# Norm factors behind W_down and on the attention scores, query chunks first in W_in, input chunks straight into yT

## The chip, the cores and the metric

The kernel runs on one core of one Trainium2 chip. The time is the device time of one execution in microseconds; the kernel before has a median of 2802.93 us over three runs (2802.38 to 2804.43).

The engines are called by short names. PE is the matrix engine (PEld is its weight load, which overlaps with the matmuls), DVE the vector engine, ACT the scalar (activation) engine, POOL the GpSimd engine, and SP the engine whose queue issues most DMA transfers. PSUM is where matmuls write, SBUF is the working memory.

## The reference

The computation is a decoder of two layers over 1024 tokens of width 1024, all in f32. In one layer:

```
a  = rmsnorm(h, norm_mix_pre)                  # y * g * rsqrt(mean(y*y) + 1e-6), per token
u  = a @ w_in                                  # 1024 -> 2640 columns, split among the heads
q, k, v, qi, ki, wi, u_conv, u_pool = split(u) # qi: 16 index heads of 64, ki: one, wi: 16 weights
idx = sum_h relu(qi_h . ki) * wi_h             # per query and key; causal; times a constant
sel = top_k(idx, 256)                          # 256 keys per query
y_attn = softmax(q . k[sel] / 8) @ v[sel]      # 8 query heads, 2 key heads
mix = concat(y_attn, conv(u_conv), pool(u_pool)) @ w_out
h += rmsnorm(mix, norm_mix_post)
m  = square(relu(rmsnorm(h, norm_mlp_pre) @ w_up)) @ w_down      # 1024 -> 4096 -> 1024
h += rmsnorm(m, norm_mlp_post)
h += sigmoid(h @ ple_gate) * (p @ ple_proj)
```

Two identities matter here. The factor r = rsqrt(mean(h*h) + eps) of a token multiplies its whole row, so it can be taken through a linear map: (r x) W = r (x W). It is positive, so relu(r x)^2 = r^2 relu(x)^2. A choice of the largest index scores of a query is not altered by a positive factor on that query's row.

## The kernel before, in words

**Layout.** Activations lie with channels in the 128 partitions and tokens along the row, 512 tokens (a "half", `hf`) at a time. Every dense product is made of three passes of 128x512 matmuls, since both operands are split into a high and a low part: `whi`/`wlo` of the weights, and the two parts of a `slot` of the activations. One "unit" is one 128-column chunk of a weight matrix against 8 slots: 24 matmuls into one of three PSUM tiles `pd` (lines 252, 257, 258). Five more PSUM tiles, `bank`, belong to attention, convolution and pooling.

**Weights.** A chunk arrives from memory as `wraw` (SP queue, 512 KB), ACT makes `whi` (L213) and POOL makes `wlo` (L214) from it.

**Phases.** The list `PHASES` runs win(0,0), win(0,1), m(0,0), win(1,0), m(0,1), win(1,1), m(1,0), m(1,1), where the pair is (layer, half). A win phase is 21 units of W_in, named in `win_order`: M0, M1, MK (mixed heads of q, k and the index weights, the rotated part), I0 to I7 (index queries; I0 and I1 carry the rotated channels), V, Q0 to Q2 (queries), A/G (convolution) and P (pooling). An m phase is W_out, a norm, W_up and W_down in four groups of 8 units each, a norm, and the embedding gate.

**Factors in a win phase.** `rms_sb` sums squares by one-column matmuls (L307), computes the factor (DVE L318, POOL power L320), spreads it over the partitions by four transposes (L312) into a `pd` tile, and ACT copies it to `rb` in SBUF (L327). Each unit's result is then multiplied by `rb`: `scaled` (L355, on DVE), the rotation tables on POOL (L344). In the first half of the first layer `rb` is needed by the very first unit's evacuation, A0 at L397.

**Factors in W_up.** After the norm that follows W_out, the squares of the new h are summed at once, four W_up units run ahead with a plain Relu on ACT, then `rms_sb` makes `rb`, the four early tiles are multiplied by it (DVE L984), and every later unit is evacuated by one DVE instruction that takes the maximum with zero and multiplies by `rb` (L990), followed by a square on ACT (L991) and a split into high and low parts.

**Temporaries.** `dtmp` is a ring of 128x512 tiles that nearly every evacuation, table, square and input chunk draws from. An input chunk of x lands in a `dtmp`, is split (L274/L275), squared (L290) and given back. `yT` holds eight 128x512 chunks in f32 and is free during the win phases of the first layer.

**Order.** Attention and convolution are generators that are advanced between units: after each unit its cost times the phase's entry in `RATES` is spent on them. Attention of a half is put on that list after unit I7; an index step loads four heads of queries at a time (L617, on POOL's queue, from the memory tensor `qiS` that the I units wrote on SP's queue at L364), multiplies them with the keys (L610) and adds relu times weight into `idx` (ACT L651, DVE L655). At the start of an m phase whatever attention of that half is left runs alone. A scheduler then puts the instructions of each engine into one fixed order by its own estimate of when they can start; each engine runs its list strictly in order, and so does each DMA queue at issue.

Of the kernel before, what the change touches and what calls it, by code (L numbers as in the profile page):

```python
# [18 lines left out]
P = 128  # L19
# [15 lines left out]
RATES = (1.205, 1.114, 0.558, 0.766, 0.751, 0.567, 0.731, 0.946)  # L35
# [14 lines left out]
def win_order(l, hf):  # L50

    return WIN_CONV + WIN_ATT if CONV_FIRST[l][hf] else WIN_ORDER
# [34 lines left out]
def tile_trunk(ctx: ExitStack, tc: tile.TileContext, xT, pT, pos, vecs, invf, cinv,  # L87
# [10 lines left out]
    class Ring:  # L98
# [8 lines left out]
        def put(self, *tiles):  # L107
            self.free.extend(tiles)
# [63 lines left out]
    wiT = const.tile([P, DEPTH, 8, 16], F32, name="wiT")  # L172
    rbs = Ring("rb", 1, [P, HALF])
# [104 lines left out]
    class Sq:  # L278
# [20 lines left out]
        def rms(self, ps, other=None):  # L299
            rms(ps, self.acc, D, 1e-6, other)  # L300
            dtmp.put(*self.acc)

    def token_sums(ps, srcs):

        for j in range(4):
            for i, src in enumerate(srcs):
                te.matmul(ps[:, j:j + 1], src[:, j * P:(j + 1) * P], ones, start=i == 0, stop=i == len(srcs) - 1)  # L307
# [6 lines left out]
    def rms(ps, srcs, n, eps, other=None):  # L314

        token_sums(other or ps, srcs)
        v = tiny("rv")
        ve.tensor_scalar(v, (other or ps)[:, :4], 1.0 / n, eps, op0=OP.mult, op1=OP.add)  # L318
        r = tiny("rr")
        gp.tensor_tensor(r, v, mhalf, op=OP.pow)  # L320
        spread(ps, r)

    def rms_sb(sq):
        ps = pd.get()
        sq.rms(ps)
        rb = rbs.get()
        sc.activation(rb, ps, AF.Copy)  # L327
        pd.put(ps)
        return rb
# [4 lines left out]
    def win_phase(l, hf, xs, sq):  # L334
        t0 = hf * HALF
        ts = slice(t0, t0 + HALF)
        rb = rms_sb(sq)

        def table(t):
            out = []  # L340
            for i in range(2):
                x = dtmp.get()
                sy.dma_start(x, tabS[2 * t + i][:, ts])
                gp.tensor_tensor(x, x, rb, op=OP.mult)  # L344
# [39 lines left out]
        for name in win_order(l, hf):  # L384
# [29 lines left out]
            elif name in ("M0", "I0"):  # L414
                held = rope_first(ps, tab, P if name == "I0" else 88)
                if name == "M0":
# [5 lines left out]
                    sc.activation(wiT[:, l, 4 * hf:4 * hf + 4], pw[:, :64].rearrange("p (j h) -> p j h", j=4), AF.Copy)  # L422
# [173 lines left out]
    def attention(l, hf):  # L596
# [43 lines left out]
        def index():  # L640

            load_k(2, 0, Ws[-1])
            for j, b in enumerate(sel):
                W = Ws[j]
                for h in range(16):
                    if h % 4 == 0:
                        q = load_q(qiS, b, h, 16)
# [120 lines left out]
        def softmax(q, b, heads, k0, ring, out):  # L768
            W = (b + 1) * P
            bias = idx[sel.index(b)] if b in sel else cbias[:, 2 * P - W:]  # L770
            for g in heads:
                t = ring.get()
                mx, nm, rs, ri = tiny("mx", 2), tiny("nm", 1), tiny("rs", 1), tiny("ri", 1)
                for n0, n1, ps in scores(q[:, g], W, k0):
# [3 lines left out]
                    banks.put(ps)  # L778
                if W > 512:
                    ve.tensor_scalar(nm, mx[:, 0:1], mx[:, 1:2], -0.125, op0=OP.max, op1=OP.mult)  # L780
                else:
                    ve.tensor_scalar(nm, mx[:, 0:1], -0.125, None, op0=OP.mult)
                s = t[:, :W]
                sc.activation(s, s, AF.Exp, scale=0.125, bias=nm, accum_out=rs)  # L784
# [80 lines left out]
    def post_norm(sq, g, ts, hsrc, gnext, fill):  # L865
# [6 lines left out]
        sq.rms(ps, sums)  # L872
# [22 lines left out]
        if gnext is not None:  # L895
            for k in reversed(range(NK)):
                nxt.add(yT[:, k])
# [36 lines left out]
    def m_phase(l, hf):  # L934
# [32 lines left out]
        rb = None  # L967
        sqy = Sq()
        for gr in range(4):
            ms = []  # L970
            for u in range(8):
                if rb is None:

                    early = []
                    for k in range(4):
                        ps, t = unit(xs, k < 2), dtmp.get()
                        sc.activation(t, ps, AF.Relu)
                        pd.put(ps)
                        early.append(t)
                    rb = rms_sb(sq)  # L980
                m = slots.get()
                if early:
                    t = early.pop(0)
                    ve.tensor_tensor(t, t, rb, op=OP.mult)  # L984
                    sc.activation(t, t, AF.Square)
                    split(m[:, 0], m[:, 1], t)
                    dtmp.put(t)
                else:
                    ps = unit(xs)
# [183 lines left out]
```

## Time and profile before

| what | value |
|---|---|
| median of three runs | 2802.93 us |
| the profiled execution, device time | 2803.82 us |
| its span (first to last instruction) | 2802.1 us |
| PE busy | 2701.1 us, 96% |
| DVE, ACT, POOL busy | 1698.4, 1599.7, 1372.7 us |
| granted PE clock over the span | 0.986 |
| bytes moved | 380.63 MB, 136 GB/s on average |

Start and end of the phases in the profiled execution: the first index score matmul of win(0,0) starts at 152.28 us, the first W_out unit that needs attention of (0,0) at 378.93 us, the last norm at about 2739 us.

A line of a waits view reads "engine tile line <- the engine, tile and line that ended the wait: us in total, times, longest". A line of a windows view reads "from:to length, PE busy (number of matmuls), then PEld, DVE, ACT and POOL in the same way, granted PE clock, share of the DMA engines, GB/s". A line of a groups view reads "line, engine, operation, out<-in, shapes, count | busy us, mean ns | idle before it, and what ended that".

### The profile page before, as it was taken

Reading aid. Unit: us, or ns where it says so; the run is one execution under the profiler, and the core shown is the slowest. Engines: PE = TensorE matmul, PEld = TensorE weight load, DVE = VectorE, ACT = ScalarE, POOL = GpSimd, SP = SyncE. Lnnn points to the kernel's source line nnn. Section 1 sums busy time; section 2 is a strip of 40 time slices with the busy share of each in tenths; the row PEclk is TensorE's granted clock in tenths of the full one; section 3 lists DMA queues with packets and bytes.
Section 4 is the critical chain, followed back from the end, with each engine's and each line's share of the span. In section 5 each row is a group of like instructions: output and inputs, shape, how many; then the busy total and the mean of one; then the engine's idle time right before and its main releaser. Section 6 shows DMA issues by size and latency. Waiting matters only on the chain.

```text
span 2802.1 us, 37352 instructions
## 1 busy us (share of the span) xinstructions
PE 2701.1 (96%) x12512; PEld 2224.5 (79%) x12512; DVE 1698.4 (61%) x3399; ACT 1599.7 (57%) x3008; POOL 1372.7 (49%) x1085
## 2 busy tenths in 40 slices
PE   8889989999999999999999989999999999999998
PEld 6678877887888787788888778788878887788886
DVE  7869668678657868784422595676785561411123
ACT  5357668776766544685633434677757664533343
POOL 4655425444334674544344764444443346544446
PEclk9999999999999999999999999999999999999999
DMA  5677555432343566543333656533222354422223
GB/s 177 203 184 226 147 140 150 109 98 84 94 109 108 185 204 192 177 128 117 90 101 103 213 156 212 155 105 110 93 85 84 105 176 150 144 98 98 98 94 132
DMA packets 193425, 380.63 MB, mean 136 GB/s; under 512 B 17232, under 2 KB 76752, under 8 KB 193232
## 3 DMA queue, kind: packets, MB, share of 16 engines
q1 hardware_dynamic: 150992, 357.26, 39.8%
q0 software_dynamic: 42240, 20.98, 4.4%
q8 instruction: 99, 1.62, 0.2%
q14 instruction: 94, 0.77, 0.1%
HBM read 305.81 MB, written 72.35 MB: 135 GB/s over the span
## 4 chain that ended last, share of the span: by engine, by line
PE 78%; DVE 10%; DMA 5%; issue 2%; ACT 2%; POOL 1%; SPq 0%; POOLq 0%; ACTq 0%; DVEq 0%
PE pd L252 22%; PE pd L257 22%; PE pd L258 22%; PE bank L610 6%; PE bank L798 2%; DVE bank L549 2%; PE bank L807 1%; PE bank L806 1%; DMA wraw<-win 1%; DVE row L761 1%; DVE dtmp L884 1%; PE pd L255 1%; PE pd L307 1%; POOL wlo L214 1%; DVE dtmp L270 1%
## 5 line engine op out<-in xcount | busy, mean ns | idle before, releaser
L214 POOL TENSOR_TENSOR wlo<-wraw,whi 128x512 fp32r<-128x512 f32 x824 | 1097.4, 1336 | 1215.7 <-ACT whi L213 1147.0
L252 PE MATMUL pd<-slot,whi 128*128 128x512 f32 x3296 | 1305.6, 397 | 44.5 <-ACT whi L213 8.9
L258 PE MATMUL pd<-slot,wlo 128*128 128x512 f32 x3168 | 1245.4, 394 | 5.4 <-POOL wlo L214 5.1
L257 PE MATMUL pd<-slot,whi 128*128 128x512 f32 x3168 | 1245.8, 393 | 0.0
L213 ACT ACTIVATE whi<-wraw 128x512 fp32r<-128x512 f32 x824 | 512.8, 627 | 722.3 <-PE pd L257 520.2
L252 PEld LDWEIGHTS pd<-slot,whi 128*128 128x128 f32 x3296 | 625.1, 190 | 181.6 <-ACT whi L213 10.8
L258 PEld LDWEIGHTS pd<-slot,wlo 128*128 128x128 f32 x3168 | 600.1, 189 | 132.6 <-POOL wlo L214 9.2
L257 PEld LDWEIGHTS pd<-slot,whi 128*128 128x128 f32 x3168 | 600.6, 190 | 121.0 <-DVE slot L275 1.2
L610 PE MATMUL bank<-kd,qst 128*128 128x512 f32 (+3 forms) x1024 | 263.4, 361 | 15.6 <-DMA qst<-qiS 6.3
L655 DVE SCALAR_TENSOR_TENSOR idx<-bank,wiT,idx 128x512 f32<-128x512 f32 (+3 forms) x300 | 190.0, 652 | 89.1 <-ACT bank L651 80.8
L610 PEld LDWEIGHTS bank<-kd,qst 128*128 128x128 f32 x1024 | 181.2, 193 | 50.5 <-DMA qst<-qiS 7.2
L651 ACT ACTIVATE bank<-bank 128x512 f32<-128x512 f32 (+2 forms) x320 | 154.6, 506 | 71.5 <-PE bank L610 69.5
L1004 DVE TENSOR_TENSOR yT<-yT,pd 128x512 f32<-128x512 f32 x96 | 65.5, 684 | 203.7 <-PE pd L258 203.1
L990 DVE SCALAR_TENSOR_TENSOR pd<-pd,rb 128x512 f32<-128x512 f32 x112 | 78.0, 696 | 166.9 <-PE pd L258 166.6
L678 DVE TENSOR_SCALAR_CACHE_REDUCE row<-row,cc 128x640 f32<-128x640 uint16 (+1 forms) x124 | 133.5, 1078 | 63.4 <-ACT row L692 56.6
L549 DVE SCALAR_TENSOR_TENSOR bank<-win,vec,bank 128x512 f32<-128x512 f32 x232 | 165.5, 746 | 7.7 <-ACT bank L547 6.0
L776 DVE CUSTOM_DVE_ANT_0 row<-bank,idx 128x512 f32<-128x512 f32 (+3 forms) x160 | 91.7, 592 | 71.4 <-PE bank L610 50.4
L692 ACT ACTIVATE row<-row,cc 128x768 f32<-128x768 uint16 (+1 forms) x124 | 121.4, 982 | 22.9 <-DVE cc L698 20.5
L270 DVE TENSOR_TENSOR cmat<-bank,cmat 128x512 fp32r<-128x512 f32 (+1 forms) x160 | 98.3, 631 | 34.5 <-ACT cmat L269 30.9
L270 DVE TENSOR_TENSOR slot<-pd,slot 128x512 fp32r<-128x512 f32 x112 | 76.8, 687 | 52.8 <-ACT slot L269 52.5
L784 ACT ACTIVATE row<-row,nmc 128x384 f32<-128x384 f32 (+5 forms) x96 | 84.1, 877 | 36.0 <-DVE nmc L780 26.7
L269 ACT ACTIVATE cmat<-bank 128x512 fp32r<-128x512 f32 (+1 forms) x160 | 83.7, 546 | 26.4 <-PE bank L798 23.1
(216 smaller groups left out, 2724.1 us busy)
## 6 DMA issues: line engine op xcount, KB each, us to landing
wraw<-wup SPq DMA_DIRECT2D x128, 512.0 KB
wraw<-wdown SPq DMA_DIRECT2D x128, 512.0 KB
wraw<-win SPq DMA_DIRECT2D x84, 512.0 KB
qiS<-dtmp SPq DMA_DIRECT2D x64, 256.0 KB
slot<-mixS SPq DMA_DIRECT2D x32, 512.0 KB
wraw<-wgate SPq DMA_DIRECT2D x32, 512.0 KB
qst<-qiS POOLq DMA_DIRECT2D x48, 256.0 KB, 3.9
hS<-yT SPq DMA_DIRECT2D x48, 256.0 KB
```

The source lines that it names most:

```text
L213: sc.activation(hi, r, AF.Copy)
L214: gp.tensor_tensor(lo, r, hi.bitcast(F32), op=OP.subtract)
L252: te.matmul(ps, wh, xh, start=i == 0, stop=False)
L257: te.matmul(ps, wh, xl, start=False, stop=False)
L258: te.matmul(ps, wl, xh, start=False, stop=i == n - 1)
L270: ve.tensor_tensor(lo, src, hi.bitcast(F32), op=OP.subtract)
L549: ve.scalar_tensor_tensor(acc[:, c] if k == TAPS - 1 else pa, src, w, pa, op0=OP.mult, op1=OP.add)
L610: te.matmul(ps[:, :n1 - n0], q, kd[:, k, k0 + n0:k0 + n1], start=k == 0, stop=k == 1)
L651: sc.activation(r, r, AF.Relu)
L655: ve.scalar_tensor_tensor(at, r, w, at, op0=OP.mult, op1=OP.add)
L678: ve.tensor_scalar(flags[:, :Ws[j]], of[j], t, None, op0=op, op1=OP.add, accum_out=dst[:, j:j + 1])
L692: sc.activation(flags[:, :Ws[j]], of[j], AF.Sign, scale=-1.0, bias=c[:, j:j + 1], accum_out=cnt[:, j:j + 1])
```

## The change

1. **Win phases.** The factor of a token is kept as a column (`rq`, tokens in partitions). Query units Q0 to Q2 and I2 to I7 are written out without it (`scaled` gone from them). The rotated tables are multiplied only in rows 64 to 88 of the M tables, which are keys, and not at all for I0/I1. The index weights `wiT` get the factor when they are transposed: four small DVE instructions instead of one on ACT. The attention scores get it as the scale of the exponential and in the row maximum, from `rq`. The index score uses unscaled index queries: a positive factor per query does not alter a choice.
2. **Order of W_in.** Units I2 and I3 (and I4 in the first phase) come first, the others in the order they had.
3. **W_up and W_down.** No `rb`: a W_up unit is evacuated by a maximum with zero alone. The squares of h are added up during the first group of W_up units, and factor powers r^2 and r^4 are computed as columns (`reciprocal`); the norm behind W_down takes them in: variance times r^4, and the final factor times r^2. The early Relu units and their four transposes are gone.
4. **Input.** The chunks of x land in `yT` instead of in `dtmp`, all eight transfers of a half ahead of the splits.
5. **Token sums.** The two accumulated tiles are summed into columns of their own and added on DVE, instead of accumulating in PSUM.
6. **Index steps.** The first query load is issued before the first index step, and two empty steps are put ahead of it. Four entries of `RATES` differ.

```diff
-RATES = (1.205, 1.114, 0.558, 0.766, 0.751, 0.567, 0.731, 0.946)
+RATES = (1.205, 1.078, 0.558, 0.775, 0.751, 0.661, 0.731, 0.94)
...
-    return WIN_CONV + WIN_ATT if CONV_FIRST[l][hf] else WIN_ORDER
+    first = ['I2', 'I3', 'I4'] if l == hf == 0 else ['I2', 'I3']
+    order = WIN_CONV + WIN_ATT if CONV_FIRST[l][hf] else WIN_ORDER
+    return first + [n for n in order if n not in first]
...
+        def reciprocal(self, ps):
+            v, r2, r4 = tiny("rv"), tiny("r2", bufs=2), tiny("r4", bufs=2)
+            variance(ps, self.acc, D, 1e-6, v)
+            dtmp.put(*self.acc)
+            ve.reciprocal(r2, v)
+            ve.scalar_tensor_tensor(r4, r2, 1.0 / D, r2, op0=OP.mult, op1=OP.mult)
+            return r2, r4
...
+    def rms(ps, srcs, n, eps, other=None, factor=None, keep=None):
         v = tiny("rv")
-        ve.tensor_scalar(v, (other or ps)[:, :4], 1.0 / n, eps, op0=OP.mult, op1=OP.add)
-        r = tiny("rr")
+        if factor is None:
+            variance(other or ps, srcs, n, eps, v)
+        else:
+            sums = other or ps
+            token_sums(sums, srcs)
+            ve.tensor_tensor(v, sums[:, :4], factor[1], op=OP.mult)
+            w = tiny("rw")
+            ve.tensor_tensor(w, sums[:, 4:8], factor[1], op=OP.mult)
+            ve.scalar_tensor_tensor(v, w, eps, v, op0=OP.add, op1=OP.add)
+        r = tiny("rr") if keep is None else keep
         gp.tensor_tensor(r, v, mhalf, op=OP.pow)
+        if factor is not None:
+            ve.tensor_tensor(r, r, factor[0], op=OP.mult)
         spread(ps, r)
...
-                gp.tensor_tensor(x, x, rb, op=OP.mult)
+                if t == 1:
+                    gp.tensor_tensor(x[64:88], x[64:88], rb[64:88], op=OP.mult)
...
-                    sc.activation(wiT[:, l, 4 * hf:4 * hf + 4], pw[:, :64].rearrange("p (j h) -> p j h", j=4), AF.Copy)
+                    for j in range(4):
+                        ve.tensor_scalar(wiT[:, l, 4 * hf + j], pw[:, j * 16:(j + 1) * 16], rq[:, l, hf, 0, j:j + 1], None,
+                                         op0=OP.mult)
...
-                put(scaled(ps), [(0, P, qiS, P * int(name[1]))])
+                put(ps, [(0, P, qiS, P * int(name[1]))])
...
-                put(scaled(ps), [(0, P, qS, P + P * int(name[1]))])
+                put(ps, [(0, P, qS, P + P * int(name[1]))])
...
+            first = load_q(qiS, sel[0], 0, 16)
+            for _ in range(2):
+                yield None
...
-                sc.activation(s, s, AF.Exp, scale=0.125, bias=nm, accum_out=rs)
+                sc.activation(s, s, AF.Exp, scale=r, bias=nm, accum_out=rs)
...
-                    ve.scalar_tensor_tensor(ps, ps, 0.0, rb, op0=OP.max, op1=OP.mult)
-                    sc.activation(ps, ps, AF.Square)
-                    split(m[:, 0], m[:, 1], ps)
-                    pd.put(ps)
+                ve.tensor_scalar(ps, ps, 0.0, None, op0=OP.max)
+                sc.activation(ps, ps, AF.Square)
+                split(m[:, 0], m[:, 1], ps)
+                if gr == 0:
+                    sq.add(yT[:, NK - 1 - u], ps)
+                pd.put(ps)
...
-            h = dtmp.get()
+            h = yT[:, k]
             sy.dma_start(h, xT[k * P:(k + 1) * P, ts])
-            if k == 0 and hf == 0:
+            if k == 1 and hf == 0:
                 ready.append(prepare(coming.pop(0)))
+        for k in range(NK):
+            h = yT[:, k]
             x = slots.get()
             xs.append(x)
             split_g(x[:, 0], x[:, 1], h, vec[:, 0, V_MIX_PRE + k:V_MIX_PRE + k + 1])
             sq.add(h)
-            dtmp.put(h)
```

The change also moves instructions. On PE, at the first unit's evacuation, the order before is the following. Lines 252, 257 and 258 are dense matmuls, 307 the sums of squares, 312 the spread of the factor; `pd_138` and `pd_139` are units A0 and G0.

```order
L307 MATMUL pd_137<-ones,dtmp_108 128x1
L257 MATMUL pd_138<-slot_82,whi_94 128x512
L258 MATMUL pd_138<-slot_82,wlo_98 128x512
L257 MATMUL pd_139<-slot_82,whi_96 128x512
L258 MATMUL pd_139<-slot_82,wlo_100 128x512
L312 MATMUL pd_137<-ident,rrd_227 128x128 x4
L252 MATMUL pd_137<-slot_75,whi_93 128x512
L257 MATMUL pd_137<-slot_75,whi_93 128x512
```

In the changed kernel (lines 255, 260, 261 are the dense matmuls, 319 the sums, 324 the spread; `pd_138` and `pd_139` are now I2 and I3) the place of the spread is this, and the sums stand behind 22 dense matmuls instead of 44:

```order
L261 MATMUL pd_139<-slot_81,wlo_100 128x512
L255 MATMUL pd_139<-slot_82,whi_96 128x512
L260 MATMUL pd_139<-slot_82,whi_96 128x512
L261 MATMUL pd_139<-slot_82,wlo_100 128x512
L324 MATMUL pd_137<-ident,rq 128x128 x4
L255 MATMUL pd_138<-slot_75,whi_95 128x512
L260 MATMUL pd_138<-slot_75,whi_95 128x512
```

Four matmuls stood between the last sum and the spread before; now there are 26, and the tile behind the spread is I2's old one, which is free without a factor.

On SP, at the start of the program, the order before is this (`wraw` is a weight chunk, `xT` an input chunk of 256 KB):

```order
L1053 DMA dtmp_102<-xT 128x512
L208 DMA wraw_91<-win 128x1024
L1053 DMA dtmp_104<-xT 128x512
L1053 DMA dtmp_106<-xT 128x512
L1053 DMA dtmp_108<-xT 128x512
L1053 DMA dtmp_101<-xT 128x512
L208 DMA wraw_92<-win 128x1024
L1105 DMA fr<-invf 128x2
L476 DMA row_121<-wcp 128x256
L208 DMA wraw_91<-win 128x1024
```

and after the change this:

```order
L1078 DMA yT<-xT 128x512 x2
L211 DMA wraw_91<-win 128x1024
L1078 DMA yT<-xT 128x512 x6
L211 DMA wraw_92<-win 128x1024
L1131 DMA fr<-invf 128x2
L511 DMA row_121<-wcp 128x256
L1078 DMA yT<-xT 128x512 x3
L211 DMA wraw_91<-win 128x1024
L1078 DMA yT<-xT 128x512 x4
```

One more chunk of x stands ahead of the first weights and eight instead of five ahead of the second; the second half's chunks, which stood among the queries' writes, now stand around the third weights, and their splits moved into the first 40 rows of ACT and DVE.

Later on SP, where the queries of the first phase are written out, the order before mixes the second half's input chunks with the writes to `qiS`:

```order
L364 DMA qiS<-dtmp_107 128x512
L364 DMA qiS<-dtmp_101 128x512
L1053 DMA dtmp_101<-xT 128x512
L364 DMA qiS<-dtmp_104 128x512
L208 DMA wraw_92<-win 128x1024
L1053 DMA dtmp_107<-xT 128x512
L364 DMA qiS<-dtmp_105 128x512
L1053 DMA dtmp_104<-xT 128x512
L1053 DMA dtmp_105<-xT 128x512
L208 DMA wraw_91<-win 128x1024
L364 DMA qiS<-dtmp_109 128x512
L364 DMA qiS<-dtmp_108 128x512
```

and now there is nothing between them but weights, with the writes of V and Q0 behind them:

```order
L397 DMA qiS<-dtmp_103 128x512
L397 DMA qiS<-dtmp_106 128x512
L211 DMA wraw_91<-win 128x1024
L397 DMA qiS<-dtmp_108 128x512
L211 DMA wraw_92<-win 128x1024
L397 DMA qS<-dtmp_101 128x512
L397 DMA qS<-dtmp_105 128x512
L492 DMA vS<-dtmp_102 128x512
```

Each input chunk stood in a queue that runs in order and had to wait for a `dtmp` to come free; now none stands there. On PE, 24 dense matmuls (unit V) lie between I7 and the first index score before, and 48 (V and Q0) after.

More of the change, by code (lines that the diff above doesn't have):

```diff
@@ L297, in add, with rms @@
             self.n += 1
-        def rms(self, ps, other=None):
-            rms(ps, self.acc, D, 1e-6, other)
+        def rms(self, ps, other=None, factor=None, keep=None):
+            rms(ps, self.acc, D, 1e-6, other, factor, keep)
             dtmp.put(*self.acc)
+        def reciprocal(self, ps):
[5 more added lines that the diff above has]
+            return r2, r4
     def token_sums(ps, srcs):
-        for j in range(4):
-            for i, src in enumerate(srcs):
-                te.matmul(ps[:, j:j + 1], src[:, j * P:(j + 1) * P], ones, start=i == 0, stop=i == len(srcs) - 1)
+        for i, src in enumerate(srcs):
+            for j in range(4):
+                te.matmul(ps[:, 4 * i + j:4 * i + j + 1], src[:, j * P:(j + 1) * P], ones, start=True, stop=True)
     def spread(ps, t4):
@@ L646, in index @@
                     if h % 4 == 0:
-                        q = load_q(qiS, b, h, 16)
+                        q = first if j == h == 0 else load_q(qiS, b, h, 16)
                     w = wiT[:, l, b, h:h + 1]
@@ L862, in attention, with post_norm @@
             yield from attend(blocks, (0, 0), rows)
-    def post_norm(sq, g, ts, hsrc, gnext, fill):
+    def post_norm(sq, g, ts, hsrc, gnext, fill, factor=None):
         side[0] = "norm"
@@ L871, in post_norm @@
         ps = pd.get()
-        sq.rms(ps, sums)
+        sq.rms(ps, sums, factor)
         pd.put(sums)
@@ L971, in m_phase @@
             for u in range(8):
[L972 to L977, printed above, removed]
-                        pd.put(ps)
-                        early.append(t)
-                    rb = rms_sb(sq)
-                m = slots.get()
[L982 to L989, printed above, removed]
-                    ve.scalar_tensor_tensor(ps, ps, 0.0, rb, op0=OP.max, op1=OP.mult)
-                    sc.activation(ps, ps, AF.Square)
-                    split(m[:, 0], m[:, 1], ps)
-                    pd.put(ps)
+                m = slots.get()
+                ps = unit(xs, gr == 0 and u < 2)
+                ve.tensor_scalar(ps, ps, 0.0, None, op0=OP.max)
[4 more added lines that the diff above has]
+                pd.put(ps)
                 ms.append(m)
                 yield 5.2
+            if gr == 0:
+                ps = pd.get()
+                apart2 = sq.reciprocal(ps)
+                pd.put(ps)
             if gr == 3:
                 slots.put(*xs)
-                rbs.put(rb)
             for o in range(NK):
```

28 lines of the change are left out of this document (16 added, 12 removed).

## The prediction

> **What bounds the kernel now.** I read the page first, then the granted clock and matmul counts of stretches, then PE's waits stretch by stretch.
>
> ```profile
> PE 2701.1 (96%) x12512; PEld 2224.5 (79%) x12512; DVE 1698.4 (61%) x3399; ACT 1599.7 (57%) x3008; POOL 1372.7 (49%) x1085
> PE 78%; DVE 10%; DMA 5%; issue 2%; ACT 2%; POOL 1%; SPq 0%; POOLq 0%; ACTq 0%; DVEq 0%
> 2500.00:2550.00 50.00, 50.00 (x222) 41.42 (x221) 9.69 (x14) 16.72 (x28) 23.89 (x19) 1.00 0.28 95
> 0.00:36.08 36.08, 23.81 (x81) 17.12 (x82) 26.28 (x48) 21.10 (x35) 14.68 (x16) 0.86 0.55 182
> 36.08:104.00 67.92, 60.20 (x248) 47.53 (x247) 63.06 (x91) 29.01 (x48) 40.37 (x32) 0.92 0.54 164
> 104.00:152.28 48.28, 38.05 (x160) 30.73 (x159) 31.78 (x48) 22.09 (x38) 25.12 (x21) 0.93 0.74 233
> 350.00:400.00 50.00, 41.76 (x189) 32.60 (x188) 31.88 (x68) 32.88 (x72) 10.32 (x11) 0.86 0.55 133
> 1050.00:1100.00 50.00, 45.75 (x196) 37.06 (x195) 49.15 (x80) 21.02 (x38) 20.63 (x18) 0.97 0.73 229
> 1650.00:1700.00 50.00, 41.89 (x171) 33.20 (x170) 42.91 (x52) 15.37 (x26) 29.34 (x23) 0.93 0.68 207
> ```
>
> PE is the bound: 96% busy, 78% of the chain. The change takes almost no matmul away, so it can only win back PE's stalls. The stretch from 2500 us is undisturbed: 222 matmuls in 50 us, 0.2252 us each, at clock 1.00. By that pace the first 152.28 us, up to the first index score, hold 81 + 248 + 160 = 489 matmuls or 110.1 us of work: 42.2 us are lost there, namely 36.08 - 81 x 0.2252 = 17.8, 67.92 - 55.8 = 12.1 and 48.28 - 36.0 = 12.3. The rows of the later win stretches show the same, smaller: 1050 loses 50 - 196 x 0.2252 = 5.9, 1650 loses 11.5. DVE's 63.06 of 67.92 and 49.15 of 50 say who sets the pace in the win phases.
>
> **Start, to 36 us.** PE's waits there, and two matmuls after the factor:
>
> ```profile
> PE pd L252 <- ACT whi L213: 7.0, 1, 7.0
> PE pd L312 <- POOL rrd L320: 3.0, 1, 3.0
> PE pd L252 <- ACT rb L327: 1.0, 1, 1.0
> 25.27 0.40 PE L258 MATMUL pd<-slot,wlo 128*128 128x512 f32 x1
> 31.38 0.63 PE L257 MATMUL pd<-slot,whi 128*128 128x512 f32 x1
> 31.81 0.63 PE L258 MATMUL pd<-slot,wlo 128*128 128x512 f32 x1
> ```
>
> Before, PE had four matmuls between the sums and the spread and then waited for POOL (3.0) and for `rb` (1.0); behind that it ran at 0.43 us a matmul instead of 0.2252 until 36.08. From 25.27 to 36.08 are 10.81 us for 16 matmuls (four spreads and twelve dense) that take 3.6 at full pace: 7.2 lost. With 26 matmuls (5.9 us) between sums and spread, and a next tile that needs no factor, that goes: -7.2.
>
> Against it: two chunks of x, not one, stand ahead of the first weights and three more ahead of the second. 0.25 MB at the row's 182 GB/s is 1.4 us, and the first transfers share with six followers; I put the first matmul 2.7 us later (bounds 1 and 4). The third weights now stand behind three chunks of the second half: 0 to 3 us, I take none, since I2 and I3 are 48 matmuls or 10.8 us of cover. Together -4.5 (bounds -6.2 and 0).
>
> [...]
>
> **Convolution and M units, 36 to 104 us.**
>
> ```profile
> PE bank L252 <- ACT cmat L269: 3.6, 1, 3.6
> PE pd L252 <- DVE dtmp L378: 1.9, 1, 1.9
> PE pd L252 <- DVE dtmp L371: 1.8, 1, 1.8
> L344 POOL TENSOR_TENSOR dtmp<-dtmp,rb 128x512 f32<-128x512 f32 x16 | 20.7, 1308 | 9.9 <-DVE bank L549 4.6 <-DMA dtmp<-tabS 3.8 <-DVE gec L697 1.0
> L355 DVE TENSOR_TENSOR pd<-pd,rb 128x512 f32<-128x512 f32 x48 | 33.2, 691 | 18.8 <-PE pd L258 18.6
> L422 ACT ACTIVATE wiT<-pd x4: 207/224/224, 67.3 to 1644.4; 128x64 f32<-128x64 f32 x4
> L318 DVE TENSOR_SCALAR rvn<-pd 128x4 f32<-128x4 f32 x8 | 1.3, 161 | 14.6 <-PE pd L307 14.6
> ```
>
> Waits of 7.3 us, the rest of the 12.1 is the clock. All wait on DVE's list (or for an ACT copy behind it). Each `scaled` is 0.69 us of DVE; 48 fall to 12, but the nine gone in this phase are those of I2 to I7 and Q0 to Q2, which ran behind 104 us, so DVE is hardly lighter here. The table multiply (1.3 us of POOL each) goes for I0/I1 and keeps its duration on 24 partitions if it goes by elements along the row (bounds 0.25 and 1.3). What is new is `wiT`: four small DVE instructions, between the 161 ns of the 128x4 row and the 224 ns of ACT's 128x64, so 0.6 to 0.9 us; they wait in DVE's in-order list behind rotation and convolution, and the `pd` tile they read is held meanwhile. That costs perhaps 1.5 us of PE in place of ACT's 0.3. The units also no longer meet convolution at the same points. I take -3.5, bounds -7 and +2.
>
> **Queries to the first score, 104 to 152 us.**
>
> ```profile
> PE bank L610 <- DMA qst<-qiS: 6.3, 1, 6.3
> PE pd L252 <- DVE dtmp L270: 3.9, 1, 3.9
> 134.14 3.06 SPq L1053 DMA_DIRECT2D dtmp<-xT  x2
> 137.93 1.05 SPq L364 DMA_DIRECT2D qiS<-dtmp  x2
> ```
>
> The first score waits 6.3 us for queries whose writes stood on SP behind input chunks that were waiting for a `dtmp` (at 134.14); PE had stalled 3.9 us for a `dtmp` just before. These two with their half clock (0.93 in the row) are most of the 12.3. Now no input chunk stands there, and V and Q0 (10.8 us) instead of V alone (5.4) run ahead of the first score. I take -10; bounds -4 (only the `dtmp` stall) and -11.
>
> **The drain ahead of m(0,0).**
>
> ```profile
> PE bank L798 <- ACT row L786: 2.5, 2, 1.5
> PE pd L252 <- DMA slot<-mixS: 2.3, 1, 2.3
> ```
>
> At 350 to 379 us attention of (0,0) ends alone: 50 - 189 x 0.2252 = 7.4 us lost in that row, though its matmuls are partly shorter. The order of the changed kernel leaves 16 more dense matmuls out of the mix in that place: 16 x 0.2252 = 3.6 us of cover gone. I take +3, bounds -1 and +6.
>
> **Second layer's win phases.**
>
> ```profile
> PE pd L252 <- ACT rb L327: 0.7, 1, 0.7
> PE pd L252 <- DVE dtmp L270: 3.4, 1, 3.4
> PE pd L252 <- ACT rb L327: 1.9, 1, 1.9
> PE pd L252 <- DVE dtmp L371: 5.0, 1, 5.0
> 1649.49 6.17 DVE L270 TENSOR_TENSOR dtmp<-dtmp,dtmp 16x512 fp32r<-16x512 f32 x1
> ```
>
> The first two are win(1,0), the next two win(1,1). The `rb` waits (0.7 and 1.9, with the half clock about 1 and 3.8) vanish as at the start. The DVE waits sit on the ring of `dtmp` and on an instruction that took 6.17 us, where wider ones take 0.69, while POOL worked; fewer `scaled` and table multiplies shift them, and I count half: 1.7 and 2.5. With the clock behind them and `wiT` +1 each: win(1,0) -3.5 (bounds -6, +1), win(1,1) -5 (bounds -9, +1).
>
> [...]
>
> **m phases.**
>
> ```profile
> L312 PE MATMUL pd<-ident,rrd 128*128 128x128 f32 x32 | 6.0, 292 | 3.0 <-POOL rrd L320 3.0
> L990 DVE SCALAR_TENSOR_TENSOR pd<-pd,rb 128x512 f32<-128x512 f32 x112 | 78.0, 696 | 166.9 <-PE pd L258 166.6
> L984 DVE TENSOR_TENSOR dtmp<-dtmp,rb 128x512 f32<-128x512 f32 x16 | 12.9, 867 | 7.6 <-ACT rb L327 7.6
> 2741.57 1.01 POOL L320 TENSOR_TENSOR rrn<-rvn,mhalf 128x4 f32<-128x4 f32 x1 [1.58 <-DVE rvn L318]
> 2744.01 0.60 PE L312 MATMUL pd<-ident,rrn 128*128 128x128 f32 x4
> ```
>
> Four groups of four spreads go: 0.60 us a group, -2.4, and I add -0.6 for the crowding around them (bounds -2 and -5). DVE's 14 us of L984 and early scaling lie beside 5.4 us units, worth nothing; a maximum for L990's maximum-and-multiply (696 ns, once per 5.4 us) likewise, with the squares of h on ACT now behind the first eight units. The factor in the norm behind W_down adds three small DVE instructions, 3 x 0.16 = 0.5 us, to the chain sums, power, spread: POOL's power ended at 2742.58 and PE, on its fill matmuls, came to the spread at 2744.01, so 1.4 us cover them. +0.5, bounds 0 and +4 (four norms without cover, 1 us each).
>
> **Sum** for the profiled execution, 2803.82 (span 2802.1 and 1.7 around it): -4.5 -3.5 -10 +3 -3.5 -5 -3 +0.5 = -26.0, so 2777.8. It stands 0.9 above the median of the runs; against the median 2776.9, and I say 2777.
>
> **Rivals.**
>
> 1. The input starves the start. 2 MB of the second half at 182 GB/s are 11 us in the first 36, and its eight splits stand on ACT and DVE (26.28 of 36 busy already) ahead of `rb`. If weights or `rb` come 7 us late, the start's -4.5 becomes +2.5 and the clock halves again (+2): 2786. For it: the DMA share of 0.55 while weights are already late. Against: 48 matmuls need no `rb`.
> 2. DVE is the bound of the win phases, and its stalls move with `wiT`. Then 36-104 gives 0, win(1,0) 0, win(1,1) -2: 2777 + 3.5 + 3.5 + 3 = 2787, up to 2791 with 1 us for each `wiT`.
> 3. Better: every win stall goes (-7, -6, -9, drain 0): 2777 - 3.5 - 2.5 - 4 - 3 = 2764.
> 4. Slower: attention starts later against its dense cover (two units ahead of it and two empty steps in each phase), so that it ends alone, as at 350 us, in all four m phases. It is 7.4 to 8.2 us of idle PE each by the row of 350 (50 - 41.76 = 8.2): 4 x 8.2 = 33, 2810. It decides from a drain of about 6.5 us in each. Against: outside the first drain the order alternates dense and attention as before.
> 5. The moves cancel within the measurement, as when 2 and half of 4 meet: about 2803.
>
> **Chances.** Forecast 0.50, input 0.13, DVE 0.16, better 0.11, slower 0.06, nothing 0.04. What a measurement of this kernel can tell is about 0.2%, 5.6 us. Faster 0.89, the same 0.05, slower 0.06. The likeliest case's own range is 2768 to 2785; the range 2759 to 2796 holds the rivals 1, 2 and 3.
>
> **What would show it.** Right: the first index score near 134 us, with no wait on `qst` and none on the spread; first matmul near 9.7. Wrong: a wait for `whi` above 3 us before 40 us (rival 1), DVE over 63 of 68 us and a wait on `wiT` or `dtmp` of more than 3 us (rival 2), an attention-only stretch longer than 30 us ahead of any m phase (rival 4), or a wait for the final factor in the norm behind W_down.

## The result

| | before | changed |
|---|---|---|
| median | 2803.68 us (4 runs, 2802.38 to 2805.08) | 2788.15 us (4 runs, 2787.85 to 2791.05) |
| ratio | 1 | 0.9944, 95% interval 0.9930 to 0.9958 |
| profiled execution, span | 2802.1 us | 2786.7 us |

The change is faster by 15.5 us. The forecast of 2777 us had the sign right and the gain too large: 26 forecast, 15.5 measured. The page of the changed kernel, its engine line, shows PE still as the bound, with 11 us less of busy time:

```profile
PE 2690.4 (97%) x12496; PEld 2218.0 (80%) x12496; DVE 1681.2 (60%) x3415; ACT 1595.4 (57%) x2982; POOL 1357.1 (49%) x1073
```

PE's waits over the whole of the changed kernel, a choice of its rows, the longest first (9.5 us of the first row are the wait ahead of the first matmul; the last row is one that was feared):

```profile
PE pd L255 <- ACT whi L216: 14.8, 8, 9.5
PE pd L261 <- POOL wlo L217: 13.5, 11, 2.8
PE bank L645 <- DVE mxc L814: 7.9, 2, 4.0
PE pd L255 <- DVE dtmp L273: 5.8, 4, 1.8
PE bank L645 <- DMA qst<-qiS: 5.5, 2, 4.6
PE pd L255 <- ACT rb L356: 0.7, 1, 0.7
PE pd L255 <- DVE wiT L456: 0.5, 1, 0.5
```

The view has no row for the spread any more, and `rb` is down to 0.7 us from 3.6; the new `wiT` instructions cost 0.5. In their place stand the weights: `wlo` 13.5 us, where the kernel before had 5.1. Stretches of the changed kernel, with as many matmuls as the stretches of the kernel before in the prediction (81, 329, 489), and the two in the second layer:

```profile
0.00:30.85 30.85, 19.49 (x81) 14.75 (x82) 23.04 (x39) 22.04 (x38) 14.24 (x16) 1.00 0.79 258
0.00:52.85 52.85, 38.32 (x150) 29.42 (x151) 42.77 (x71) 32.60 (x56) 21.58 (x22) 0.94 0.69 234
0.00:96.60 96.60, 80.23 (x329) 63.70 (x330) 82.79 (x130) 51.20 (x84) 51.03 (x45) 0.95 0.57 190
0.00:138.65 138.65, 117.98 (x489) 92.81 (x490) 121.24 (x184) 70.58 (x119) 74.51 (x63) 0.96 0.62 201
1050.00:1100.00 50.00, 47.63 (x208) 38.08 (x207) 49.73 (x80) 21.86 (x41) 25.07 (x20) 1.00 0.70 231
1650.00:1700.00 50.00, 47.33 (x204) 37.84 (x204) 43.67 (x61) 18.80 (x33) 33.26 (x24) 1.00 0.72 229
```

The kernel before needed 36.3 us for 81 matmuls and 51.95 for 150:

```profile
0.00:36.30 36.30, 24.03 (x81) 17.34 (x82) 26.46 (x49) 21.32 (x35) 14.68 (x16) 0.86 0.55 181
0.00:51.95 51.95, 39.68 (x150) 30.28 (x151) 38.99 (x67) 32.71 (x53) 21.23 (x21) 0.90 0.51 169
```

So 5.5 us are won by the 81st matmul, all of it is given back by the 150th (52.85 against 51.95), and then some is won again. The table counts matmuls in the trace and gives when the next one starts; the last rows count dense matmuls, whose number is the same in both kernels, so that phases can be compared:

| where | before | changed | difference |
|---|---|---|---|
| first matmul | 7.01 | 9.53 | +2.5 |
| after 81 matmuls | 36.35 | 30.88 | -5.5 |
| after 150 | 52.00 | 52.91 | +0.9 |
| after 329 | 104.46 | 96.67 | -7.8 |
| after 520 (first scores done) | 160.55 | 151.11 | -9.4 |
| after 1400 (before the drain) | 345.90 | 334.38 | -11.5 |
| m(0,0), first unit after W_out | 413.17 | 403.86 | -9.3 |
| win(1,0) | 944.15 | 937.40 | -6.8 |
| m(0,1) | 1080.02 | 1073.67 | -6.4 |
| win(1,1) | 1593.91 | 1590.31 | -3.6 |
| m(1,0) | 1735.28 | 1719.16 | -16.1 |
| m(1,1) | 2328.93 | 2313.70 | -15.2 |
| gate of m(1,1), first unit | 2747.55 | 2732.15 | -15.4 |

Each column is one execution, and small differences in it mean little. Four kernels of the experiments below (factor back in W_up, no early query load, old RATES, first query load on SP) run the same instructions in the same order as the changed kernel on every engine up to the first query load. Yet their 329th matmul starts at 94.2, 97.8, 95.5 and 93.1 us, where the changed kernel's starts at 96.7. A difference of up to 5 us at that place needs no edit to explain it.

### The profile page after: what moved, and what is told of

Its sections match the earlier page's. It is cut to its first block, busy times and chain, and to the rows that moved or that the text cites. A ratio compares the mean times of both kernels' runs of the same rounds, so it can differ in the third digit from the quotient of the medians.

```text
span 2786.7 us, 37259 instructions
## 1 busy us (share of the span) xinstructions
PE 2690.4 (97%) x12496; PEld 2218.0 (80%) x12496; DVE 1681.2 (60%) x3415; ACT 1595.4 (57%) x2982; POOL 1357.1 (49%) x1073
## 4 chain that ended last, share of the span: by engine, by line
PE 78%; DVE 11%; DMA 5%; issue 3%; ACT 2%; POOL 2%; SPq 0%; POOLq 0%; DVEq 0%; ACTq 0%
PE pd L255 22%; PE pd L261 22%; PE pd L260 21%; PE bank L645 6%; DVE bank L584 2%; PE bank L837 2%; DMA kd<-kS 1%; PE bank L846 1%; DMA wraw<-win 1%; PE bank L845 1%; POOL wlo L217 1%; DVE row L799 1%; PE pd L258 1%; PE pd L319 1%; DVE dtmp L923 1%
## 5 line engine op out<-in xcount | busy, mean ns | idle before, releaser
L261 PE MATMUL pd<-slot,wlo 128*128 128x512 f32 x3168 | 1240.9, 393 | 13.8 <-POOL wlo L217 13.5
L1010 DVE TENSOR_SCALAR pd<-pd 128x512 f32<-128x512 f32 x128 | 89.0, 697 | 163.8 <-PE pd L261 162.5
L273 DVE TENSOR_TENSOR slot<-pd,slot 128x512 fp32r<-128x512 f32 x128 | 87.8, 687 | 68.7 <-ACT slot L272 68.4
L297 DVE TENSOR_TENSOR dtmp<-dtmp,pd 128x512 f32<-128x512 f32 x88 | 60.2, 684 | 108.3 <-ACT pd L293 108.1
L823 ACT ACTIVATE row<-row,nmc,rq 128x384 f32<-128x384 f32 (+5 forms) x96 | 93.0, 969 | 23.5 <-DVE nmc L819 18.0
```

What stands on the lines that cost most here:

```text
L261: te.matmul(ps, wl, xh, start=False, stop=i == n - 1)
L273: ve.tensor_tensor(lo, src, hi.bitcast(F32), op=OP.subtract)
```

## Where the start's gain went

ACT's timeline in the changed kernel, between the copy of `rb` and the next weights (`whi`):

```profile
27.14 0.59 ACT L356 ACTIVATE rb<-pd 128x512 f32<-128x512 f32 x1
36.71 1.28 ACT L200 ACT_TABLE_LOAD   x1 [8.98 <-issue]
38.00 0.64 ACT L200 ACTIVATE dtmp<-dtmp 128x512 f32<-128x512 f32 x1
39.06 1.13 ACT L216 ACTIVATE whi<-wraw 128x512 fp32r<-128x512 f32 x2
```

DVE's timeline there (L278 are splits of the second half's input, L194 to L199 the angles of the rotation tables):

```profile
26.99 1.75 DVE L278 SCALAR_TENSOR_TENSOR slot<-yT,vec,slot 128x512 fp32r<-128x512 f32 x1
28.67 1.51 DVE L194 TENSOR_SCALAR dtmp<-dtmp,fr 128x512 f32<-128x512 f32 x1
30.10 1.40 DVE L278 SCALAR_TENSOR_TENSOR slot<-yT,vec,slot 128x512 fp32r<-128x512 f32 x2
36.23 0.41 DVE L199 TENSOR_SCALAR dtmp<-dtmp 128x512 f32<-128x512 f32 x1
```

And PE's:

```profile
38.59 0.39 PE L261 MATMUL pd<-slot,wlo 128*128 128x512 f32 x1
40.25 0.50 PE L255 MATMUL pd<-slot,whi 128*128 128x512 f32 x1 [1.27 <-ACT whi L216]
42.87 0.79 PE L261 MATMUL pd<-slot,wlo 128*128 128x512 f32 x1 [1.90 <-POOL wlo L217]
43.47 0.63 PE L255 MATMUL pd<-slot,whi 128*128 128x512 f32 x1
43.89 0.63 PE L260 MATMUL pd<-slot,whi 128*128 128x512 f32 x1
```

ACT did nothing from 27.7 to 36.7 us: the next instruction in its list was the sine of the rotation tables, and the angle was clipped on DVE (L199) only at 36.23. (The row of the table load names no releaser. The clip ends at 36.64 us, and in the trace ACT stands at a semaphore that DVE raises until 36.68.) The high part of the next weights stood behind the sine, PE ran out of them, and at 43.47 it ran at half pace (0.42 us apart, granted clock 0.50 from 43 to 48 us). My reading: the second half's splits, now early because their input needs no temporary, delay the angles. The rival, the first of the prediction: the transfers of the second half make the weights late.

**Splits held.** The transfers stay early; only the splits wait.

```diff
+        g = vec[:, 0, V_MIX_PRE:V_MIX_PRE + 8]
+        if hf == 1:
+            late = const.tile([P, 8], F32, name="late")
+            ve.scalar_tensor_tensor(late, wiT[:, 0, 0, :8], 0.0, g, op0=OP.mult, op1=OP.add)
+            g = late
-            split_g(x[:, 0], x[:, 1], h, vec[:, 0, V_MIX_PRE + k:V_MIX_PRE + k + 1])
+            split_g(x[:, 0], x[:, 1], h, g[:, k:k + 1])
```

> The changed kernel, with the splits of the second half's input chunks held until the index weights exist (a tiny DVE instruction makes their scale from them); the transfers stay where they are. Theory: the 7 us that the changed kernel gives back between the 81st matmul (30.88 us) and the 150th (52.91 us) come from these splits: they stand on DVE among the angles of the rotation tables, ACT waits 9 us in front of the first sine, and the weights' high parts are queued behind it. Then the 150th matmul starts at 46 to 48 us, ACT's wait in front of the first sine (L200) is under 4 us, and the whole is 2782 to 2787 us, since the splits cost up to 4 us where they go. Rival: the 2 MB of the second half make the weights land late; then the 150th matmul stays at 52 to 54 us and the whole at 2788 us or more.

Measured: 2783.21 us (2780.09 to 2788.91), ratio to before 0.9928 (0.9908 to 0.9948). ACT's timeline in front of the first sine of this kernel, then the stretch of its first 150 matmuls and a later one:

```profile
31.06 1.28 ACT L200 ACT_TABLE_LOAD   x1 [2.29 <-issue]
```

```profile
0.00:47.80 47.80, 36.73 (x150) 28.32 (x151) 35.34 (x58) 26.87 (x46) 20.26 (x20) 0.96 0.69 237
80.00:125.00 45.00, 33.50 (x121) 24.83 (x120) 44.15 (x65) 16.30 (x27) 26.30 (x19) 0.85 0.45 138
```

The next after 150 matmuls starts at 47.84 us, as the theory said (50.7 to 52.9 in the changed kernel and the four with its order), with the transfers where they were, issued from 9.7 to 19.3 us (10.2 to 19.9 in the changed kernel): the place of the splits is the cause, not the transfers. But from 80 to 125 us only 121 matmuls run, where the changed kernel has 167:

```profile
80.00:125.00 45.00, 40.12 (x167) 31.23 (x166) 43.76 (x64) 15.82 (x28) 28.44 (x22) 0.96 0.59 178
```

DVE is full there in both kernels (44.15 and 43.76 of 45 us), and with the splits held it has the splits to do as well. Between the 150th and the 520th matmul this kernel goes from 5.1 us ahead of the changed one to 1.7 us behind it: the held splits cost some 7 us there, more than the 4 expected. The first index score comes later than in the changed kernel (146.2 against 144.0 us). The interval of the whole overlaps the changed kernel's, so a gain is not shown.

**Second half through temporaries again.**

```diff
-            h = yT[:, k]
+            h = yT[:, k] if hf == 0 else dtmp.get()
+            if hf == 1:
+                sy.dma_start(h, xT[k * P:(k + 1) * P, ts])
...
+            if hf == 1:
+                dtmp.put(h)
```

> The changed kernel, with the second half's input chunks in the ring of temporaries again, as before the change; the first half still lands in yT. Both the theory of the splits and the rival of the transfers expect the 150th matmul at 46 to 48 us here. What tells is the other end: the wait for a temporary and the late query writes should come back, 4 to 10 us before the first index score, so that the whole is 2784 to 2793 us. If the late wait does not come back, landing in yT was worth nothing and the whole is about 2781 us.

Measured: 2794.01 us, ratio 0.9960 (0.9949 to 0.9972), 1 us above the range expected. The next after 150 matmuls starts at 48.98 us, so here too the loss at the start is gone. The late end came back as expected: the first index score at 150.4 us, behind these two waits between 110 and 165 us.

```profile
PE pd L255 <- DVE dtmp L273: 3.2, 1, 3.2
PE bank L645 <- DMA qst<-qiS: 2.5, 1, 2.5
```

## The first index score

**First query load on SP.** In the changed kernel, SP issued the last write of the index queries, POOL's next instructions were these, and then came the score:

```profile
131.45 0.40 SPq L397 DMA_DIRECT2D qiS<-dtmp  x1
134.22 0.15 POOL L427 MEMSET win<- 128x60 f32 x1 [1.27 <-DVE bank L584]
135.50 1.67 POOL L594 TENSOR_TENSOR ctmp<-row 128x512 f32<-128x512 f32 x1 [1.13 <-DVE row L584]
137.13 1.26 POOL L217 TENSOR_TENSOR wlo<-wraw,whi 128x512 fp32r<-128x512 f32 x1
138.34 1.72 POOL L652 DMA_DIRECT2D qst<-qiS  x2
144.02 2.93 PE L645 MATMUL bank<-kd,qst 128*128 128x384 f32 x8 [4.58 <-DMA qst<-qiS]
```

```diff
-        def load_q(src, b, h0, nh):
+        def load_q(src, b, h0, nh, sp=False):
...
+            if sp:
+                sy.dma_start(x.bitcast(F32), v[:, h0:h0 + 4, b * P:(b + 1) * P])
+            else:
+                gp.dma_start(x, v[:, h0:h0 + 4, b * P:(b + 1) * P])
...
-            first = load_q(qiS, sel[0], 0, 16)
+            first = load_q(qiS, sel[0], 0, 16, True)
```

> The changed kernel, with only the first index query load of each attention taken off POOL's queue and put on SP's. Theory: the first index score waits 4.6 us because POOL came to that load at 138.3 us, behind two of its instructions that waited for convolution on DVE. Then the wait is under 1.5 us and the whole 2784 to 2787 us. Rival: the last write of the index queries (issued at 131.45 us) had not landed; then the wait stays above 3.5 us and the whole at 2787 to 2789 us.

Measured: 2774.74 us (2774.13 to 2778.20), ratio 0.9898 (0.9881 to 0.9915): clearly faster than both kernels, and by more than either theory said. The issue of the first load, what SP's queue had waited for before it (between 120 and 145 us: in total, times, longest), and the score:

```profile
134.52 0.37 SPq L653 DMA_DIRECT2D qst<-qiS  x1
SPq L653 <- DMA qiS<-dtmp: 5.6, 2, 4.8
138.38 0.98 PE L645 MATMUL bank<-kd,qst 128*128 128x384 f32 x2 [2.50 <-DMA qst<-qiS]
```

The wait is 2.5 us, between the two expectations, but the first theory fails: SP itself stood 4.8 us until the last write of the queries had landed. By the landing times in the trace this write, issued at 131.45 us in the changed kernel, landed at 137.47, and POOL issued the load 0.9 us later; here it was issued at 128.32, landed at 134.38, and SP issued the load 0.1 us later. So POOL's list held less than 1 us. The load itself then took 5.6 us to land there and 3.7 here; why is not settled, since loads on POOL's queue took 3.3 us in other kernels (splits held, for one).

This explains little of the gain of 13 us. In the profiled executions (span 2776.2 against 2786.7) 1.3 us lie before the first matmul and 2.3 more before the 329th, where both kernels run the same instructions in the same order, so the edit did not make them. Behind the first score the scheduler's order is another one (PE's list differs at 1,106 of 12,496 places). PE loses 6.2 us less in m(0,0): the wait of 4.0 us for the selection (`mxc`, first layer) is not there, and the drain is 3.5 us shorter. That wait is also absent with the splits held and with the second half through temporaries, where the loads are on POOL's queue, so it goes with the order and not with the queue. The edit moves four loads, one for each attention; whether the queue or the new order gains the 13 us is not settled.

**Both cures.** The two edits together:

> The changed kernel with both cures: the splits of the second half held until the index weights exist, and the first index query load on SP's queue. Taken alone the first brought 5 us and the second 13. If they cure different waits, 2768 to 2774 us; if the second only escaped the first's trouble, or the held splits fill DVE just ahead of the queries, 2774 to 2784 us.

Measured: 2782.60 us, ratio 0.9931 (0.9914 to 0.9948), on the second expectation: with the splits held the first score is late whichever queue loads it (146.3 us, and 146.2 with POOL's), and the gain of the query load is lost. That the one is the cause of the other is not shown: the old order of W_in and the DVE multiplications, below, have their first score as late (146.0 and 145.8 us), with 2792.36 and 2785.21 us.

## Which part of the change is worth what

**Old order of W_in**, all else as changed:

```diff
-    first = ['I2', 'I3', 'I4'] if l == hf == 0 else ['I2', 'I3']
+    first = []
```

> The changed kernel with the old order of W_in (no query units first), all else as changed. If the order is what hides the factor at the start, the waits on the spread and on rb come back there (3.0 and 1.0 us and the half clock behind them, some 7 us) and at the starts of the second layer's win phases (about 1 and 4 us): 2796 to 2802 us. If the factor was hidden by something else, 2786 to 2792 us.

Measured: 2792.36 us, ratio 0.9957 (0.9945 to 0.9968). The waits came back at the start, in this kernel's waits of the first 110 us:

```profile
PE pd L324 <- POOL rq L347: 3.4, 1, 3.4
PE pd L255 <- ACT rb L356: 0.7, 1, 0.7
```

and 81 matmuls took 36.2 us. Yet after 150 it stands at 51.89, where the changed kernel stands at 52.91: by then nothing of the order's gain is left. What undoing the order costs stands later in its profile, in win(0,1), where PE loses some 10 us against 3. In all it costs about 4 us, not the 8 to 14 expected, and the intervals overlap.

**DVE multiplications back** (by 1.0, so nothing else changes; the same line ahead of Q's write), and **table multiplications back** on POOL:

```diff
+                ve.tensor_scalar(ps, ps, 1.0, None, op0=OP.mult)
                 put(ps, [(0, P, qiS, P * int(name[1]))])
...
                 if t == 1:
                     gp.tensor_tensor(x[64:88], x[64:88], rb[64:88], op=OP.mult)
+                else:
+                    gp.tensor_tensor(x, x, ones.to_broadcast([P, HALF]), op=OP.mult)
```

> The changed kernel with a DVE multiplication by 1.0 put back on each query unit's PSUM tile (I2 to I7 and Q0 to Q2, 36 instructions of about 0.7 us), where the multiplications by the factor stood before. If DVE is what sets the pace of the win phases, these 25 us of DVE work cost PE a good part: the unexpectedly large gain of win(1,1) (lost time 16.6 to 7.0 us) shrinks by 3 us or more, and the whole is 2794 to 2800 us. If DVE is not the bound there, the whole stays within 3 us of the changed kernel's 2788.

> The changed kernel with POOL's multiplication of the two rotation tables of the index queries put back (by one, 8 instructions of 1.3 us). Theory: before, PE waited 5.0 us in win(1,1) for a rotated tile (L371) that stood behind such a multiplication; then lost time in win(1,1) goes from 7.0 to 11 us or more and the whole to 2791 to 2795 us. Rival: the gain came from elsewhere (DVE, or the factor's place); then the whole stays at 2786 to 2790 us.

Measured: 2785.21 us, ratio 0.9935 (0.9914 to 0.9956), and 2787.49 us, ratio 0.9944 (0.9924 to 0.9963). Neither differs from the changed kernel. The first has 25 us more DVE work than the changed kernel on its page,

```profile
PE 2688.6 (97%) x12496; PEld 2213.6 (80%) x12496; DVE 1706.5 (61%) x3451; ACT 1599.0 (57%) x2982; POOL 1357.1 (49%) x1073
```

and no microsecond of it shows in the whole. PE loses about 7 and 6 us in win(1,1), against 7.0 in the changed kernel. Each alone, these multiplications were off the path; both together were not put back.

**Factor back in W_up**, **no early query load**, **old RATES**:

```diff
-            first = load_q(qiS, sel[0], 0, 16)
-            for _ in range(2):
-                yield None
...
-RATES = (1.205, 1.078, 0.558, 0.775, 0.751, 0.661, 0.731, 0.94)
+RATES = (1.205, 1.114, 0.558, 0.766, 0.751, 0.567, 0.731, 0.946)
```

(each in a kernel of its own; the first puts back the lines of W_up that the change took out).

> The changed kernel with the norm factor applied in W_up as before (four early units, the spread, the multiplication in each unit), all else as changed. The prediction put this part at -2.5 us (16 spreads of PE and 0.5 us of longer chain): 2789 to 2793 us. If the squares in the first group or the chain behind W_down cost something, undoing it gains: 2782 to 2787 us.

> The changed kernel without the early load of the first index queries and the two empty steps ahead of the index. If these are what let the first score come late without harm, the first index score's wait grows from 4.6 us to 8 us or more and each later attention start waits for its queries: 2791 to 2797 us. If POOL's queue is the hindrance anyway, the load comes as late either way and the whole is 2786 to 2791 us.

> The changed kernel with the four old entries of RATES. Theory: the longer drain ahead of m(0,0) (lost time in the W_out part 18.2 us before, 22.9 after) comes from the entry of win(0,1), by which less attention runs beside the dense units; then it returns to 18 to 20 us, and the whole is 2783 to 2788 us. Rival: the drain is longer because attention started later against the dense units; then it stays at 22 us or more and the whole is 2787 to 2793 us.

Measured: 2787.21 us, ratio 0.9938 (0.9914 to 0.9962); 2789.84 us, ratio 0.9946 (0.9928 to 0.9965); 2788.33 us, ratio 0.9944 (0.9928 to 0.9961). None can be told from the changed kernel, and the last two edits test less than they were meant to. Without the early load every engine runs the same instructions in the same order as in the changed kernel up to 1705 us, POOL, which issues the query loads, to the end: the scheduler put the first load in the same place without it (the first score waits 4.5 us), so this run says nothing of what an early load is worth. With the old RATES the lists are the same up to 768 us. The time that PE loses in the W_out part of m(0,0), by its matmuls against their usual pace, is 21.7 us against 22.9 with the same instructions in the same order, which is scatter: the entry of win(0,1) accounts for nothing of the 4.8 us by which it grew.

**Factors only**: old order, old landing of both halves, old RATES; the early query load and the new token sums stay in it. **Landing only**: the kernel before with this one part.

```diff
-            h = dtmp.get()
+            h = yT[:, k]
             sy.dma_start(h, xT[k * P:(k + 1) * P, ts])
-            if k == 0 and hf == 0:
+            if k == 1 and hf == 0:
                 ready.append(prepare(coming.pop(0)))
+        for k in range(NK):
+            h = yT[:, k]
...
-            dtmp.put(h)
```

> The changed kernel with the old order of W_in, the old landing of the input chunks (both halves in temporaries) and the old RATES: what is left is the norm factors' new places and the early index queries. Undoing the order cost 4 us and undoing the second half's landing 6; if the parts add up, the factors alone are worth some 5 us and this is 2796 to 2800 us. If the factors' new places are worth nothing by themselves, it is 2801 to 2806 us; if they are the main thing, under 2794 us.

> The kernel before with one part of the change alone: the input chunks land in yT. By the experiment that undid it for the second half (6 us), 2795 to 2799 us. The late wait for the queries (6.3 us) and for a temporary (3.9 us) should be gone, and the splits among the angles should cost something at 30 to 50 us, as in the changed kernel. If the landing needs the new order to be worth anything, 2800 us or more.

Measured: 2805.14 us, ratio 1.0007 (0.9994 to 1.0020), and 2820.16 us, ratio 1.0053 (1.0032 to 1.0073). The factors' new places alone are worth nothing in sum. By phase, the profile gains some 9 us in win(1,1) and 5 in m(1,0) and loses 3 each in win(0,0) and the drain and 4 each in win(1,0) and the W_out part of m(0,1). The landing alone makes the kernel slower, although the two late waits went as expected (1.6 us on the queries in place of 6.3, none for a temporary) and its first index score comes 6.6 us earlier (145.6 against 152.3 us): the profile has lost that lead by the end of the drain and is 9 us behind at the end of m(0,0). (The profiled execution, 2811.4 us, is the shortest of its five runs, so the profile shows only part of what the median lost.) In m(0,0), right behind its first norm, PE's longest wait is this:

```profile
445.63 1.22 PE L255 MATMUL pd<-slot,whi 128*128 128x512 f32 x2 [3.42 <-DVE slot L275]
```

against 0.99 in the kernel before. The longest of the whole phase is one for the selection (`mxc`), 5.4 us against 0.7. The parts do not add up: undoing the order alone costs 4 us and the second half's landing alone 6, each with an interval that overlaps the changed kernel's; undoing them together with the first half's landing and RATES costs 17 (2805.14 against 2788.15).

## The second layer, and what moved there

Win(1,1) gave 12.5 us against the 5 forecast, win(1,0) gave nothing against 3.5. A pile-up stood in the first in the kernel before, the 6.17 us instruction of the prediction; the changed kernel has its like in win(1,0), on DVE, among these on POOL:

```profile
1008.48 6.54 DVE L273 TENSOR_TENSOR dtmp<-dtmp,dtmp 88x512 fp32r<-88x512 f32 x2 [3.52 <-ACT dtmp L272]
```

```profile
1007.74 1.30 POOL L412 TENSOR_TENSOR dtmp<-dtmp,dtmp 88x512 f32<-88x512 f32 x1
1008.99 1.29 POOL L551 TENSOR_TENSOR row<-row 128x512 f32<-128x512 f32 x1
1010.24 1.29 POOL L594 TENSOR_TENSOR ctmp<-row 128x512 f32<-128x512 f32 x1
1011.49 5.92 POOL L217 TENSOR_TENSOR wlo<-wraw,whi 128x512 fp32r<-128x512 f32 x4
```

One of the two splits in that DVE row took 4.85 us. Of the kernels run, the only two with a DVE instruction above 4 us in win(1,1) are the two with the old factors, before (6.17) and landing only (6.15), and they alone lose more than 15 us there; all others lose 6 to 9. In win(1,0) eight of them have one (4.8 to 6.5 us), and it is not seen to cost PE time: these eight lose 11 to 15 us there, and so do the others. So the gain in win(1,1) goes with the factors' new places in the win phases and the new token sums, since all twelve kernels that have these show it, with the old order of W_in, the old landing and the old RATES too. Which instruction of theirs makes it is not settled: neither multiplication, put back alone, brings the pile-up back to win(1,1).

The slow DVE rows here (6.17 us in the kernel before, 4.85 us in the changed one) read two tiles in SBUF while POOL computes beside them throughout. In the kernel before, splits of that kind (L275, `slot<-yT,vec,slot`) have a median of 0.74 us where POOL computes nothing beside them (9 of 48) and 1.33 us where it computes throughout (20 of 48), while splits with one tile in PSUM (L270, `slot<-pd,slot`) take 0.69 us in both cases. What makes the first kind slower beside POOL is not shown.

## Why the prediction came out as it did

- **Start, -4.5.** Right at the 81st matmul: -5.5, with the first matmul 2.5 us later (2.7 forecast) and no wait on the spread. What failed is the sentence that the second half's transfers and splits cost nothing because I2 and I3 are 48 matmuls of cover: the cover was for the factor, not for the sine in front of the next `whi`. 6.4 us were given back between 38 and 48 us, as rival 1 had it, but through DVE's and ACT's lists and not through the transfers.
- **Convolution and M units, -3.5.** From the 81st to the 329th matmul -2.3, in a sum of the loss above and later gains; the four kernels with the same instructions there give -0.2 to -5.0, so the term is neither confirmed nor refuted.
- **Queries to the first score, -10.** This is the step that failed by most: from the 329th to the 520th matmul only -1.7. The input chunks did leave SP's queue there and the 3.9 us wait went, but the first score, forecast near 134 us without a wait, came at 144.0 us after a wait of 4.6. The step left out a chain that freeing SP's queue does not shorten: the last write of the queries has to land (6.0 us) before the load is issued, and the load has to land (5.6 us). From the issue of the last write to the score passed 13.6 us before and 12.6 now; the write came 7.2 us earlier, and V and Q0 did not cover the rest.
- **Drain, +3.** From 1400 matmuls to the next unit behind W_out +2.2.
- **Second layer's win phases, -8.5 together.** Measured +0.4 and -12.5; the m phase between them lost 2.8. That the sum is near is luck: one phase gave nothing and the other more than twice its term. Of the half clock that the term counts behind both `rb` waits, the kernel before shows it behind the second alone (matmuls 0.43 us apart from 1609.83 to 1612.82 us, 1.7 us lost by 1613.19); behind the first, of 0.7 us, the granted clock is 1.00 (957 to 966 us). The `rb` wait of win(1,1) fell from 1.9 to 0.7 us, and the pile-up on DVE went, but neither multiplication that the term counted on brings it back when put back alone.
- **m phases, -2.5.** PE's work is 1.7 us less by the 16 spreads (forecast 2.4), the chain behind W_down is covered as said, and putting the factor back changes nothing measurable. m(0,0) behind the drain cost 2.5 us that no term held, 3.1 of it lost in the third W_down group, where the wait for the selection is.
- **Rival 2** (DVE as the bound): 25 us of DVE work put back cost nothing. At the start it was the place of DVE's work in its list that counted, not its amount. **Rival 4**: PE's lost time in the W_out part grew by 4.8 us in m(0,0), by 2.4 in m(0,1), where it is a wait for `wlo`, and not in the other two.

## What to carry to other kernels

Giving the input its own buffer took away a wait here (3.9 us for a `dtmp`), and with it the thing that kept its later work late: ask what such work will stand in front of once it is free to start, on each engine's list and one engine further on (DVE's angles, ACT's sine, the weights). When a load reads what was just written, count the whole chain, the write's landing, the load's issue and its landing (12.6 us here), before putting its wait down to a queue. An edit that lets a scheduler order the instructions anew changes more than the line edited, or nothing at all: compare the lists of instructions of the two profiles first, since moving four loads changed PE's order behind them and brought 13 us, and two other edits left it the same over the stretch they were meant to test. Parts of a change are not worth their sum: test them alone and left out, since here one part was worth nothing, one made it slower, and together they gained 15 us. How they do it together is not shown.

## Unexpected in the hardware

In the changed kernel PE ran at half pace (matmuls 0.43 us apart) behind two waits of 1.27 and 1.90 us within four microseconds (PE's rows from 38.59 on), neither as long as the wait of 3.0 us at the start of the kernel before, and again behind a single wait of 1.84 us that ended at 86.09 us (granted clock 0.50 from 86.1 to 89.5). A DVE instruction took 6.17 us on 16 partitions (kernel before, at 1649.49 us) and 4.85 us on 88 (changed kernel, at 1008.48 us) beside a run of POOL instructions, where the shortest of the same line and size took 0.69 and 0.68.
